# A fourth outer product by seven quarter products: spilled operands, smaller result pieces, half-tile loads

## The chip, the cores and the metric

The kernel runs on one core of one Trainium2 chip. The metric is the device time of one execution in microseconds (us); before the change the median of three runs is 1509.48 us.

## The reference

```python
def reference(x, w):                       # x: 8 x 2048 x 2048 f32, w: 2048 x 2048 f32
    cs = np.cumsum(x, axis=1)
    diff = cs - np.concatenate([zeros((B, 1, D)), cs[:, :-1, :]], axis=1)
    return np.matmul(diff, w).astype(np.float32)
```

The difference of the running sum is x itself, so what has to be computed is x times w: 16384 rows by 2048 times 2048 by 2048.

## The kernel before, in words

The 16384 rows are 128 tiles of 128 rows. The first four tiles are multiplied plainly in bf16 while w is loaded (lines 207 to 389). The other 124 are taken in 31 groups of four: tiles g, g+1, h = g+2 and h+1. A tile of x is loaded by SP (`bring`, line 97), measured by ACT with an absolute sum (`measure`, `weigh`, `weigh_in`), scaled to f16 in place by ACT (`narrow`, line 114), and transposed by a DMA that SP starts (`turn_over`, line 124), whole for even tiles and by two halves for odd ones.

Within a group two levels of Winograd's form of Strassen's scheme are at work.

- The outer level takes the row pair (g, g+1) as the two row halves of a 2 x 2 block product, with K and N halved to 1024. Its seven products are A11 x B11, A12 x B21, S4 x B22, A22 x T4, S1 x T1, S2 x T2 and S3 x T3. S1 to S4 are sums of blocks of x, made by DVE (`total`, line 510) in f16; T1 to T4 are differences of blocks of w, made once. The pair (h, h+1) has the same products. A product of one pair is 16 matmuls of 128x128 by 128x512, so a product for both pairs is 32.
- The inner level takes one outer product for both pairs at once, g and h being its two row halves of 128 rows, and cuts K and N again to 512. It needs seven quarter products of 4 matmuls instead of eight: 28 matmuls in place of 32. Its operands on the side of x are made by DVE each group (`sums_in`); those on the side of w are made once and kept in SBUF (`less_in`, tile `inner`, the lists Q1 to Q4 and t11 to t22).

Before the change three of the seven outer products are made by quarter products in groups 2 to 31: A12 x B21 (`in2`), S4 x B22 (`in3`) and A22 x T4 (`in4`). Four are direct: 4 x 32 + 3 x 28 = 212 matmuls in a group. The first group (`group_plain`) makes all seven directly, 224.

PSUM has eight banks of 128x512. A product is gathered in a bank and then taken out, scaled by its row's factor, into a piece of the result in SBUF: the first one by ACT (`keep`, line 497), the others added by DVE (`add`, line 502). Before, such a piece is 128x1024 f32 and there are four of them (`new_c`); a finished one is stored by SP (`put`, line 507). ABS passes of ACT throw their elementwise output into a free piece (line 105) or a bank (line 553).

The order of each engine's instructions is the order of the program text: `after` (line 134) ties every ACT, DVE and SP instruction behind the last one asked for on the same engine. Matmuls of the groups are asked for without `after`, and stand in the order of the text too. PE writes a bank again only when the instruction that takes it out is done; that wait is a semaphore.

Of the kernel before, what the change touches and what calls it, by code (L numbers as in the profile page):

```python
# [7 lines left out]

# [3 lines left out]
def kernel(  # L34
# [31 lines left out]
    KQ = KO // 4  # L66

    x2 = x.rearrange("b s d -> (b s) d")
    out2 = out.rearrange("b s d -> (b s) d")


# [11 lines left out]
    wmax = const.tile([P, 2 * KO], f32, name="wmax")  # L83
    wred = const.tile([P, 1], f32, name="wred")
# [3 lines left out]
    fin = ctx.enter_context(tc.tile_pool(name="fin", bufs=2))  # L88
    small = ctx.enter_context(tc.tile_pool(name="small", bufs=6))
    xtpool = ctx.enter_context(tc.tile_pool(name="xT", bufs=2))  # L90
# [4 lines left out]


    def bring(t):
        xf = fin.tile([P, K], f32, name="fin")
        return xf, nc.sync.dma_start(xf, x2[ds(t * P, P), :])

    def measure(xf, waste):
        m = small.tile([P, 1], f32, name="m")
        return m, nc.scalar.activation(  # L105
            waste.bitcast(f16), xf, ABS, scale=1.0 / ROW, accum_out=m
        )

    def invert(m):
        s = small.tile([P, 1], f32, name="s")  # L110
        nc.vector.tensor_scalar(m, m, TINY, None, MAX)  # L111
        return s, nc.vector.reciprocal(s, m)  # L112

    def narrow(xf, s):
        xh = xf.bitcast(f16)[:, :K]
        return xh, nc.scalar.activation(xh, xf, COPY, scale=s)  # L116


    def place(t):
        if t % 2 == 0:  # L120
            return [xtpool.tile([P, KO, P], f16, name="xT")]
        return [xtpool.tile([P, KH, P], f16, name=f"xT{h}") for h in range(2)]

    def turn_over(xT, xh):
        n = K // len(xT)
        return [
            nc.sync.dma_start_transpose(a, xh[:, ds(i * n, n)])
            for i, a in enumerate(xT)
        ][-1]

# [12 lines left out]

    with tc.tile_pool(name="ring", bufs=7) as ring, tc.tile_pool(
        name="o", bufs=7
    ) as opool, tc.tile_pool(name="first", bufs=1) as first:
        xP = first.tile([P, PLAIN, KO, P], bf16, name="xP")
        eye = first.tile([P, P], bf16, name="eye")
        zeros = xP[:, 0, :KQ, :].rearrange("p k m -> p (k m)")

# [74 lines left out]

# [19 lines left out]
        def plain_out(h, r):  # L245
            for n in here(h, r):
                if h == 0 or r > 0:
                    c = opool.tile([P, NB], f32, name="o")
                else:
                    c = ring.tile([P, NH], bf16, name="wb").bitcast(f32)  # L250
                after("act", lambda: nc.scalar.copy(c, ps[r][n]))
                done.append((c, ds(r * P, P), ds(h * NH + n * NB, NB)))
# [66 lines left out]
        x4, _ = after("sp", lambda: bring(PLAIN))  # L319
        x6, _ = after("sp", lambda: bring(PLAIN + 2))  # L320
# [23 lines left out]

        waste = first.tile([P, NH], f16, name="waste")
        got = {}
        scales = {}

        def measure_2(t, xf):
            m, m2 = (small.tile([P, n], f32, name=i) for n, i in ((1, "m"), (2, "m2")))  # L350
            for i in range(2):
                at = ds(i * NH, NH)
                after(
                    "act",
                    lambda: nc.scalar.activation(
                        waste, xf[:, at], ABS, scale=1.0 / ROW, accum_out=m2[:, i : i + 1]
                    ),
                )
            after("dve", lambda: nc.vector.tensor_reduce(m, m2, AX.X, ADD))
            scales[t], _ = after("dve", lambda: invert(m))  # L360
            got[t] = m, None

        def narrow_turn(t, xf):
            xh, _ = after("act", lambda: narrow(xf, scales[t]))
            xT = place(t)
            got[t] = got[t][0], xT
            return after("sp", lambda: turn_over(xT, xh))
# [25 lines left out]
        measure_2(PLAIN, x4)  # L393
        for k in range(4, KH):
            block(B11, 0, 0, k, "dve")
        narrow_turn(PLAIN, x4)
# [3 lines left out]
        measure_2(PLAIN + 2, x6)  # L400
        finish_row(1)
        there = xP.rearrange("p r k m -> p (r k m)")
        x5 = there[:, : 2 * K].bitcast(f32)
        after("sp", lambda: nc.sync.dma_start(x5, x2[ds((PLAIN + 1) * P, P), :]))
        narrow_turn(PLAIN + 2, x6)
# [7 lines left out]
        for c, rows, columns in done:  # L413
            after("sp", lambda: put(c, rows, columns, nc.sync))
        m = small.tile([P, 1], f32, name="m")
        after(
            "act",
            lambda: nc.scalar.activation(
                there[:, ds(2 * K, K)].bitcast(f16), x5, ABS, scale=1.0 / ROW, accum_out=m
            ),  # L420
        )
        scales[PLAIN + 1], _ = after("dve", lambda: invert(m))
        got[PLAIN + 1] = m, None
        narrow_turn(PLAIN + 1, x5)
        x7, _ = after("sp", lambda: bring(PLAIN + 3))
# [23 lines left out]

    S1, S2, S4g, S4h, S0 = (Part(B12[j]) for j in range(5))  # L450
    cpool = ctx.enter_context(tc.tile_pool(name="C", bufs=1))
    inpool = ctx.enter_context(tc.tile_pool(name="inner", bufs=1))
    inner = inpool.tile([P, 30, NB], f16, name="inner")
    spare = [inner[:, j, :] for j in range(30)]
    spare += [B12[k][:, n, :] for k in range(5, KH) for n in range(2)]


    def quarters(b):
        return *([spare.pop() for _ in range(4)] for _ in range(3)), *(
            [t[:, n, :] for t in b[4 * a : 4 * a + 4]] for a in range(2) for n in range(2)  # L460
        )

    in2, in3, in4 = quarters(B21), quarters(B22), quarters(T4)

    def product(ps, a, b, first):
        for k in range(KH):
            for n in range(NH // NB):
                nc.tensor.matmul(  # L468
                    ps[n],
                    a[k],  # L470
                    b[k][:, n, :],
                    start=(first and k == 0),
                    stop=(k == KH - 1),
                    skip_group_check=True,
                )

    def product_in(ps, a, b, first):
        for k in range(4):
            nc.tensor.matmul(  # L479
                ps, a[k], b[k], start=(first and k == 0), stop=(k == 3), skip_group_check=True  # L480
            )

    def both(ps):
        return ps.unsqueeze(1).to_broadcast([P, 2, NB])

    def halves(c):
        return c.rearrange("p (n c) -> p n c", c=NB)


    def pieces_of(dst, ps):  # L490
        if isinstance(ps, list):
            return [(dst[:, ds(n * NB, NB)], ps[n]) for n in range(2)]
        return [(dst, ps)]

    def keep(dst, ps, scale):
        for c, p in pieces_of(dst, ps):
            after("act", lambda: nc.scalar.activation(c, p, COPY, scale=scale))  # L497

    def add(dst, ps, scale):
        for c, p in pieces_of(dst, ps):  # L500
            after(
                "dve", lambda: nc.vector.scalar_tensor_tensor(c, p, scale, c, MUL, ADD)  # L502
            )

    def put(c, t, h):
        after(
            "sp", lambda: nc.sync.dma_start(out2[ds(t * P, P), ds(h * NH, NH)], c)
        )

    def total(dst, p, q, op):  # L510
        after("dve", lambda: nc.vector.tensor_tensor(dst.all, p.all, q.all, op))  # L511
# [5 lines left out]

    def less_in(Q1, Q2, Q4, t11, t12, t21, t22):
        less(Q1, t12, t11)
        less(Q2, t22, Q1)  # L520
        less(Q4, t21, Q2)

    def less_in3(Q1, Q2, Q4, t11, t12, t21, t22):
        less(t12, t22, t12)

    def new_c(slot):
        return cpool.tile([P, NH], f32, name=f"c{slot}")

    END = M // P
    came = {PLAIN + 3: x7}  # L530
    units = {}

    def fetch_x(t):
        if t < END:
            came[t], _ = after("sp", lambda: bring(t))

    def weigh(t, slot):
        if t < END:
            xf = came.pop(t)
            m, _ = after("act", lambda: measure(xf, new_c(slot)))  # L540
            got[t] = m, None, xf


    def weigh_in(t, ps):
        if t < END:
            xf = came.pop(t)
            m = small.tile([P, 1], f32, name="m")
            m4 = small.tile([P, 4], f32, name="m4")
            for i in range(4):
                at = ds(i * NB, NB)  # L550
                after(
                    "act",
                    lambda: nc.scalar.activation(  # L553
                        ps[i % 2],
                        xf[:, at],
                        ABS,
                        scale=1.0 / ROW,
                        accum_out=m4[:, i : i + 1],
                    ),
                )  # L560
            after("dve", lambda: nc.vector.tensor_reduce(m, m4, AX.X, ADD))  # L561
            got[t] = m, None, xf

    def scale_of(t):
        if t < END:
            m, _, xf = got[t]
            s, _ = after("dve", lambda: invert(m))
            came[t] = xf, s
# [373 lines left out]
```

## Time and profile before

| | |
|---|---|
| median of 3 runs (lowest, highest) | 1509.48 us (1509.03, 1510.4) |
| span of the profiled execution | 1507.3 us (the profile gives no other time for that execution) |
| matmuls | 6911, PE busy 1490.6 us |
| DVE busy | 1104.4 us in 2053 instructions |
| ACT busy | 864.5 us in 1107 instructions |
| DMA | 351.50 MB, mean 233 GB/s; the hardware queue of SP 81.1% of 16 engines' time |
| HBM read, written | 150.99 MB, 134.22 MB |
| transposes by DMA | 186, started by SP; 5.2 us from start to landing |

A busy time is the union of an engine's instructions; starting a transfer isn't counted as busy on the engine that starts it, but it holds that engine's queue. A group of instructions is written as line, engine, operation, output<-input. In a row of the timeline the first two numbers are the start and the time taken, in us from the span's start.

### The profile page before, as it was taken

What the parts mean: (1) busy time and instruction counts of PE and PEld (TensorE: products, weight loads), DVE (VectorE), ACT (ScalarE), POOL (GpSimd) and SP (SyncE); (2) the same over time, 40 slices, a digit from 0 to 9 for tenths busy, and PEclk for the clock granted to TensorE, in tenths of its full rate; (3) what the DMA queues carried; (4) which work ended last, traced back from release to release, by engine and by line L of the source; (5) the groups of instructions that cost most, each with busy time, mean ns of one, the idle gap of its engine ahead of it and who ended that gap; (6) DMA issues with size and microseconds to landing.
All of it is one profiled execution on the core that took longest, in us unless ns stands there. A gap on an engine that the chain in (4) does not pass through costs nothing.

```text
span 1507.3 us, 19123 instructions
## 1 busy us (share of the span) xinstructions
PE 1490.6 (99%) x6911; PEld 673.8 (45%) x6911; DVE 1104.4 (73%) x2053; ACT 864.5 (57%) x1107; POOL 5.2 (0%) x12
## 2 busy tenths in 40 slices
PE   8999999999999999999999999999999999999998
PEld 3444444444444444444444444444444444444443
DVE  7997777776677676777676776766776767776767
ACT  5875655565655566555656555655555565556551
POOL 0100000000000000000000000000000000000000
PEclk9999999999999999999999999999999999999999
DMA  9988878878978987888789788878788888887772
GB/s 362 351 250 233 236 224 246 234 213 227 235 225 244 224 224 236 215 246 236 210 229 232 230 241 217 235 222 248 216 244 207 236 221 250 232 236 216 223 208 112
DMA packets 322479, 351.50 MB, mean 233 GB/s; under 512 B 266896, under 2 KB 266896, under 8 KB 306512
## 3 DMA queue, kind: packets, MB, share of 16 engines
q1 hardware_dynamic: 321536, 347.92, 81.1%
q0 software_dynamic: 560, 1.84, 0.3%
q8 instruction: 54, 0.88, 0.2%
q10 hardware_dynamic: 288, 0.52, 0.1%
q14 instruction: 41, 0.34, 0.1%
HBM read 150.99 MB, written 134.22 MB: 189 GB/s over the span
## 4 chain that ended last, share of the span: by engine, by line
PE 88%; DVE 1%; DMA 1%; issue 0%; ACT 0%; DVEq 0%; ACTq 0%; SPq 0%
PE b L468 52%; PE b L479 36%; DVE c L502 1%; DMA fin<-in_x_dram 0%; DMA xT<-fin 0%; DVE W L511 0%; ACT b L553 0%; DVE W L515 0%; ACT c L497 0%; DVEq L937 0%; DVE xT L511 0%; DVE s L112 0%; DVE m L111 0%; DVE u L586 0%; DVE m L561 0%
## 5 line engine op out<-in xcount | busy, mean ns | idle before, releaser
L502 DVE SCALAR_TENSOR_TENSOR c<-b,u,c 128x512 f32<-128x512 f32 (+1 forms) x883 | 675.0, 799 | 234.8 <-ACT c L497 112.8
L497 ACT ACTIVATE c<-b,u 128x512 f32<-128x512 f32 x496 | 314.5, 680 | 265.4 <-PE b L468 170.5
L468 PE MATMUL b<-W,xT 128*128 128x512 f16 x2048 | 462.1, 379 | 0.8 <-ACT c L497 0.8
L468 PE MATMUL b<-W,W 128*128 128x512 f16 x1764 | 411.7, 379 | 1.8 <-ACT c L497 1.5
L105 ACT ACTIVATE c<-fin 128x2048 f16<-128x2048 f32 x92 | 175.7, 1910 | 242.4 <-DMA out_dram<-c 220.5
L468 PEld LDWEIGHTS <-xT 128*128 128x128 f16 x2048 | 200.4, 98 | 242.6 <-issue 1.1
L468 PEld LDWEIGHTS <-W 128*128 128x128 f16 x2016 | 197.2, 98 | 240.2 <-issue 2.1
L116 ACT ACTIVATE fin<-fin,s 128x2048 f16<-128x2048 f32 x123 | 246.3, 2002 | 93.8 <-issue 50.8
L479 PEld LDWEIGHTS <-W 128*128 128x128 f16 x1560 | 152.1, 98 | 187.5 <-issue 2.5
L479 PE MATMUL b<-W,W 128*128 128x512 f16 x810 | 220.0, 379 | 1.0 <-DVE c L502 1.0
L479 PE MATMUL b<-W,xT 128*128 128x512 f16 x720 | 180.0, 379 | 0.0
L479 PE MATMUL b<-inner,W 128*128 128x512 f16 x660 | 176.2, 379 | 0.0
L479 PEld LDWEIGHTS <-xT 128*128 128x128 f16 x960 | 93.9, 98 | 113.3
L561 DVE TENSOR_REDUCE m<-m 128x1 f32<-128x4 f32 x29 | 4.6, 157 | 106.7 <-ACT b L553 106.7
L553 ACT ACTIVATE b<-fin 128x512 f32<-128x512 f32 x116 | 67.8, 585 | 14.5 <-DMA fin<-in_x_dram 14.5
L468 PE MATMUL b<-W 128*128 128x512 f16 x252 | 75.0, 379 | 0.0
L511 DVE TENSOR_TENSOR W<-W,xT 128x1024 f16<-128x1024 f16 x122 | 68.2, 559 | 3.2
L511 DVE TENSOR_TENSOR W<-xT,W 128x1024 f16<-128x1024 f16 x122 | 67.5, 553 | 0.0
L479 PE MATMUL b<-inner,xT 128*128 128x512 f16 x240 | 61.6, 379 | 0.0
L233 PE MATMUL b<-wb,xP 128*128 128x512 bf16 x240 | 55.4, 383 | 5.9 <-ACT wb L216 4.8
L511 DVE TENSOR_TENSOR W<-xT,xT 128x1024 f16<-128x1024 f16 (+1 forms) x92 | 54.8, 596 | 0.0
L111 DVE TENSOR_SCALAR m<-m 128x1 f32<-128x1 f32 x124 | 18.5, 149 | 34.6 <-ACT c L105 33.5
(54 smaller groups left out, 457.9 us busy)
## 6 DMA issues: line engine op xcount, KB each, us to landing
out_dram<-c SPq DMA_DIRECT2D x247, 512.0 KB, 3.1
fin<-in_x_dram SPq DMA_DIRECT2D x123, 1024.0 KB, 5.5
W<-in_w_dram SPq DMA_DIRECT2D x32, 512.0 KB, 9.6
W<-in_x_dram SPq DMA_DIRECT2D x16, 256.0 KB, 7.4
xT<-fin SPq DMA_TRANSPOSE x184, 5.2
out_dram<-o POOLq DMA_DIRECT2D x7, 256.0 KB, 3.9
out_dram<-o SPq DMA_DIRECT2D x7, 256.0 KB, 4.1
xP<-in_x_dram SPq DMA_DIRECT2D x1, 1024.0 KB, 5.1
```

Of the source, the lines that this page charges most:

```text
L105: return m, nc.scalar.activation(waste.bitcast(f16), xf, ABS, scale=1.0 / ROW, accum_out=m)
L111: nc.vector.tensor_scalar(m, m, TINY, None, MAX)
L116: return xh, nc.scalar.activation(xh, xf, COPY, scale=s)
L233: lambda: nc.tensor.matmul(ps[r][n], xP[:, r, ko, :], wb[h, ko][:, ds(n * NB, NB)], start=(ko == 0), stop=(ko == KO - 1),),
L468: nc.tensor.matmul(ps[n], a[k], b[k][:, n, :], start=(first and k == 0), stop=(k == KH - 1), skip_group_check=True,)
L479: nc.tensor.matmul(ps, a[k], b[k], start=(first and k == 0), stop=(k == 3), skip_group_check=True)
L497: after("act", lambda: nc.scalar.activation(c, p, COPY, scale=scale))
L502: "dve", lambda: nc.vector.scalar_tensor_tensor(c, p, scale, c, MUL, ADD)
L511: after("dve", lambda: nc.vector.tensor_tensor(dst.all, p.all, q.all, op))
L553: lambda: nc.scalar.activation(ps[i % 2], xf[:, at], ABS, scale=1.0 / ROW, accum_out=m4[:, i : i + 1],),
L561: after("dve", lambda: nc.vector.tensor_reduce(m, m4, AX.X, ADD))
```

## The change

- From group 4 on (28 groups, `five` in the code), S1 x T1 is also made by seven quarter products (`in_5`): 3 x 32 + 4 x 28 = 208 matmuls. Groups 2 and 3 still have three such products, and their quarter products are ordered anew.
- The operands on the side of w no longer fit: four lists of four quarters (Q4 of the products 2, 4 and 5, and t21 of product 3) lie in DRAM (`spill`) and pass through one buffer `flow` (128x2048 f16, 512 KB), brought four times in a group by SP (`bring_flow`). Four inner operands on the side of x pass through `passing`; several others take the place of blocks that are no longer needed.
- The result is held in seven pieces of 128x512 f32 instead of four of 128x1024; each is stored by itself, 16 stores of 256 KB a group instead of 8 of 512 KB.
- x is loaded by halves into a tile `F` of five halves (8 loads of 512 KB a group instead of 4 of 1 MB), measured and scaled by halves, and transposed by halves; the transposes are started by ACT (`turn`) instead of SP.
- Quarter products, steps of two contraction blocks of S2 x T2 and S3 x T3 (`go(P6g)`, `go(P7g)`) and evictions are interleaved in a new order, and matmuls are tied by `after` as well.

The core of the diff, with the new helpers and the new group (X and Y are two banks each, q, e, v and w one each):

```diff
+queue_of_x = [PLAIN, PLAIN + 2, PLAIN + 3]
+for t in range(PLAIN + 4, END, 4):
+    queue_of_x += [t, t + 2, t + 1, t + 3]
+for i, t in enumerate(queue_of_x):
+    where[t] = [F[:, i % 3, :], F[:, 3 + i % 2, :]]
...
+def turn(t, halves=range(2)):
+    if t < END:
+        for i in halves:
+            after(
+                "act",
+                lambda: nc.scalar.dma_start_transpose(
+                    place(t)[i], narrowed(t)[:, ds(i * NH, NH)]
+                ),
+            )
...
-inner = inpool.tile([P, 30, NB], f16, name="inner")
+inner = inpool.tile([P, 24, NB], f16, name="inner")
+flow = inpool.tile([P, 4, NB], f16, name="flow")
+spill = [spills.tile([P, 4, NB], f16, name=f"spill{i}") for i in range(4)]
+free = [cpool.tile([P, NB], f32, name=f"c{i}") for i in range(7)]
...
+def bring_flow(i):
+    after("sp", lambda: nc.sync.dma_start(flow, spill[i]))
...
+def put(c, t, at):
+    after("sp", lambda: nc.sync.dma_start(out2[ds(t * P, P), ds(at * NB, NB)], c))
+    free.append(c)
...
+product(X, A11g, B11, True)            # slots 0 to 3
...
+keeps(C11g, X, ug)
+product(Y, A11h, B11, True)            # 4 to 7
+keeps(C11h, Y, uh)
+weigh(next_g)
+quarter(q, a11, Q.t11, True)           # 8
+add(C11g[0], q, ug)
+quarter(e, s1, Q.Q1, True)             # 9
+add(C11h[1], e, uh)
+quarter(v, a12, Q.t21, True)           # 10
...
+quarter(q, s2, Q.Q2, False)            # 11
+add(C11g[1], q, ug)
+quarter(e, s4, Q.t22, False)           # 12
+add(C11g[1], e, ug)
...
+total(S1h, A21h, A22h, ADD)
+total(S3h, A11h, A21h, SUB)
+scale_of(next_g)
+narrow(next_g)
+total(S2h, S1h, A11h, SUB)
+go(P6g, 2)                             # 13, 14
+quarter(q, s3, Q.Q3, False)            # 15
...
+weigh(next_h)
...
+go(P6g, 2)                             # 16, 17
+keeps(C12g, X, ug)
+turn(next_g, [0])
+quarter(q, a22, Q.Q4, False)           # 18
+add(C11h[0], q, uh)
+put(C11h[0], h, 0)
+bring_flow(3)
...
+scale_of(next_h)
+narrow(next_h)
...
+go(P6h, 4)                             # 19 to 22
+keeps(C12h, Y, uh)
...
+go(P7g)                                # 23
+quarter(v, a12, N.t21, True)           # 24
+keep(C22g[0], v, vg)
+quarter(q, a11, N.t11, True)           # 25
...
+weigh(next_k)
+go(P7g)                                # 26
+quarter(w, b11, R.t11, True)           # 27
+add(C12g[0], w, ug)
+quarter(v, b12, passed, False)         # 28, passed lies in flow
+bring_flow(1)
...                                     # 29 to 43
+quarter(w, r3, R.Q3, False)            # 44
...
+quarter(q, a11, Q.t11, True)           # 45
+keep(C21g[0], q, vg)
+turn(next_h, [1])
+quarter(X[0], a12, Q.t21, False)       # 46
...
+narrow(next_l, [0])
+quarter(e, s1, Q.Q1, True)             # 47
+keep(C21g[1], e, vg)
+keep(C21h[1], e, vh)
+narrow(next_l, [1])
+quarter(X[1], s4, Q.t22, False)        # 48
+turn(next_k, [1])
+turn(next_l, [0])
+quarter(q, s2, Q.Q2, False)            # 49
+add(C21g[1], q, vg)
+add(C21g[1], X[1], vg)
+put(C21g[1], g + 1, 1)
+add(C21h[1], Y[1], vh)
+quarter(Y[0], a22, Q.Q4, False)        # 50
+keep(C21h[0], Y[0], vh)
+quarter(q, s3, Q.Q3, False)            # 51
+add(C21h[1], q, vh)
...
+turn(next_l, [1])
```

The numbers behind the matmul lines are counted here in fours of matmuls from the group's first one.

## The prediction

> **What bounds the kernel now.** I read the engine table first, then the chain, then one steady group by window, its waits, and the queue that starts the transfers.
>
> ```profile
> PE 1490.6 (99%) x6911; PEld 673.8 (45%) x6911; DVE 1104.4 (73%) x2053; ACT 864.5 (57%) x1107; POOL 5.2 (0%) x12
> PEclk9999999999999999999999999999999999999999
> DMA  9988878878978987888789788878788888887772
> ...
> PE 88%; DVE 1%; DMA 1%; issue 0%; ACT 0%; DVEq 0%; ACTq 0%; SPq 0%
> ```
>
> PE fills the span and carries 88% of the chain; its clock is granted in full. So only a matmul removed, or a wait added on PE, can move the time. Windows of one group of four row tiles (columns: busy us and count by engine, clock, DMA share, GB/s):
>
> ```profile
> 726.62:772.42 45.80, 45.80 (x213) 20.69 (x212) 32.95 (x62) 26.24 (x35) 0.00 (x0) 1.00 0.85 227
> 1413.62:1459.42 45.80, 45.80 (x213) 20.76 (x212) 32.95 (x62) 26.23 (x35) 0.00 (x0) 1.00 0.80 239
> ```
>
> Every group takes 45.80 us for 212 matmuls, with no PE idle: 0.216 us a matmul. DVE has 12.9 us to spare, ACT 19.6, DMA 15 to 20%. These are what the change spends. Now SP's queue in that group, which starts the transposes today:
>
> ```profile
> 742.64 3.23 SPq L127 DMA_TRANSPOSE xT<-fin  x1
> ...
> 750.04 4.41 SPq L127 DMA_TRANSPOSE xT<-fin  x1
> ...
> 765.59 2.98 SPq L127 DMA_TRANSPOSE xT<-fin  x2
> ...
> 774.23 1.99 SPq L127 DMA_TRANSPOSE xT<-fin  x1
> ```
>
> Starting a transpose holds the queue for 1.2 to 5.2 us (median 1.95 over the run; 463 us in all, 15 a group). Lastly the end of the last group, where PE does wait:
>
> ```profile
> 1499.28 2.07 DVE L502 SCALAR_TENSOR_TENSOR c<-b,u,c 128x512 f32<-128x512 f32 x3 [0.81 <-PE b L479]
> ...
> 1501.40 0.38 PE L479 MATMUL b<-W,W 128*128 128x512 f16 x1 [0.50 <-DVE c L502]
> ```
>
> The last quarter product adds onto bank q, so it waits until DVE has read q; one other quarter product lies between.
>
> **Part 1, matmuls removed: -24.2 us.** In 28 of the 31 groups S1 x T1 for both row pairs falls from 32 matmuls to 28 (the instruction orders agree: 6911 to 6799). All of them lie on the path: 112 x 0.216 = 24.2. A quarter product (4 matmuls, 0.864 us) is my unit below, "slot"; such a group shrinks from 53 slots to 52, 44.9 us. I count slots from its first matmul.
>
> **Part 2, the one-slot gap on q: +0.14 us a group.** Each group now ends as the old last one did: S2 onto q (slot 49), Y0 (50), S3 onto q (51). From rows: DVE starts 0.42 us after the start of the last matmul before it (743.53 to 743.95), takes 0.75, and PE follows 0.05 after it (1501.35 to 1501.40): 1.22. Undisturbed, PE would start after 5 matmuls, 1.08. So 0.14 a group even with DVE free. In the old tail two queued adds made it 0.5. In the other places I find two slots or more between a read and the next write of a bank.
>
> **Part 3, ACT.** Sixteen evictions a group stay (0.60 us apart, 9.6). ABS by halves: 1.18 each (60.65 to 61.83 in the start), 8 make 9.4; scaling by halves about 1.1 (the 128x1024 ACTIVATE of line 341 is 1.14), 8.8. Together 27.8, against 26.2 now. New are 8 half transposes to start. A half with nothing queued ahead took 1.23 to 1.65; the second of a pair behind two 512 KB stores 3.1 to 4.4. I take 1.4, since ACT's own ring holds nothing but transposes and most of the eight stand 3 us or more apart: 11 us. That is 39 of 44.9. Part of it hides: ACT's queue runs ahead of its arithmetic (the wait for line 116 began at 745.45, the pass before it ran to 747.25), so a transpose can be started while the instruction before it still computes. What is queued behind a transpose is the point, at two places:
>
> - Slots 13 to 28. e's second quarter ends at slot 13 (11.4 us with the 0.42), DVE adds it (12.2), forms two sums (0.61 apart) and the scale: 13.9. ACT scales tile g+4 (to 16.1), measures h+4 (18.4), evicts C12g (19.6; PE wants that bank at slot 23, 19.9), starts a transpose from 18.5 to 19.9, scales h+4 (20.0 to 22.2), evicts C12h (23.5) and v (24.1). PE writes v again at slot 28, 24.2. Margin 0.1; I charge 0.1.
> - Slots 46 to 51. Evict q (39.9 to 40.6), transpose (39.95 to 41.35), half a scaling (42.4), evict e into C21g (43.0). DVE's add of q to the same C21g can begin at 43.35 (slot 50). Margin 0.35, so with 1.4 us the wait stays that of part 2; I charge 0.06 for scatter.
>
> With part 2: 0.30 us a group, 28 x 0.30 = 8.4. Bounds: 0 (if the ends of matmuls are modelled late) and, with a transpose start of 3.2, 0.14 + 1.45 = 1.6 at the second place alone.
>
> A rule here: "DMA: Bandwidth & Descriptors" in the Trainium skill, section "Issuing engines are not separate DMA queues", holds that the time to initiate a DMA "is usually small relative to the DMA itself". By it the moved starts would cost ACT nothing worth counting and the sum would lose the 0.16 us of part 3, 4.5 us in all. The trace disagrees for transposes: median 1.95 us on the queue, 5.1 to landing.
>
> **Part 4, DVE.** 35 adds (0.71 apart by the group's 18.4 us for 26), 8 sums of 1024 (5.5), 16 of 512 (0.40, 6.4), 12 small ones (1.9): 38.6 of 44.9, from 32.95. The closest place is the add of e (C12h0) before slot 47: a run of adds from 28.7 us ends at 40.2, PE wants e at 40.56. Nothing charged; if that cover fails, each 0.1 us is 2.8 us.
>
> **Part 5, transfers.** A group moves 4 x 512 KB more through the flow buffer, 2.1 MB on 10.5. Mean packet times in the trace: 8192 B 430 ns, 4096 B 169, 2048 B 92, transposes' 256 B 25. Today: 512 x 430 + 1024 x 169 + 8192 x 25, over 16 engines, 37 us. After: x by halves 1024 x 169, C 2048 x 92, transposes as now, flow 512 x 169: 10.8 + 11.8 + 12.7 + 5.4 = 40.7, 0.91 of the group. The tightest is the flow before slot 28: its buffer is free at slot 19, issue about 17.4, wanted at 24.2, 6.8 us; loads and stores land in 3.1 to 5.5 today. The seven C pieces are each reused at least 3 us after their store starts. Nothing charged. SP's 28 plain starts take 0.33 each, 9 us; a transpose's wait on ACT no longer blocks them, but loads wait there for transposes to land, about 6.7 us into the next group, before the first store is due (10.4).
>
> A rule that speaks against the change: the same page, "Rules for kernel authors", wants at least 1 MiB per DMA for bandwidth. By it all pieces here are too small and the DMA share would rise past 0.91. The packet rows say the reverse for x: two of 4096 B take 338 ns, one of 8192 B 430.
>
> **Part 6, start and three unconverted groups: +2 us (0 to 6).** Sixteen half transposes move to ACT in the first 130 us (1.24 to 1.4 each, about 20 us), where ACT is busy about 70% of the time (66.4 us of the first 90) and PE already waited 2.3 us for its evictions.
>
> **Sum.** From the profiled span: 1507.3 - 24.2 + 8.4 + 2 = 1493.5. The median of the runs, 1509.48, lies 2.2 us over that span (the execution's own time beside its span is not in the profile); I carry that: 1495.7, say 1496.
>
> **Rivals.**
> - *Everything is hidden* (the waits of parts 2 and 3 vanish into DVE's and ACT's slack): 1509.5 - 24.2 + 0.5, about 1486. For it: all budgets fit. Against: the 1.22 us of part 2 stand in the rows.
> - *ACT's transposes take PE's place as the bound* (slower): if a start on ACT lasts 3.2 us, as many do on SP, the eviction of e at slot 48 is late and PE loses 1.6 us a group against 0.86 gained: 1509.5 + 2 + 28 x 0.74 = 1532. It decides from 0.14 + (t - 1.75) = 0.79, t = 2.4 us. For it: median start 1.95, many at 3 to 4.4 now. Against: those had plain transfers ahead of them on the same queue.
> - *Flow late* (slower): if a 512 KB flow lands in 9.6 us, as W's loads did when DMA was 0.98 busy, PE loses 2.8 us a group: 1509.5 + 2 + 28 x 1.94 = 1566. Against: 0.91, not 0.98, and landings of 3.1 to 5.5 at 0.85.
>
> That the change does not do what it says is excluded by the count of matmuls.
>
> **Chances.** Forecast 0.50 (its own range 1489 to 1505), all hidden 0.20, ACT 0.22 (1507 to 1550), flow 0.08. A measurement here can tell about 0.2%, 3 us, from no change. Faster: 0.48 + 0.20 + 0.02 (a mild ACT case) = 0.70; same: 0.02 + 0.03 + 0.01 = 0.06; the rest, 0.24, slower. Range 1485 to 1526: it leaves out half of the ACT case, most of the flow case and a little below, 0.2 in all.
>
> **What would show it.** Right: groups of 44.9 to 45.5 us, 208 matmuls each; PE idle on the DVE adder just before each group's last quarter; transposes on ACT's queue near 1.4 us; DVE busy near 38.6, DMA near 0.9. Wrong: PE waiting on evictions by ACT, with starts over 2.4 us; PE's first flow quarter waiting for a DMA; or groups over 45.8 us for any reason.

## The result, and the profile after

The changed kernel takes 1808.5 us (median of 4 runs, 1798.89 to 1816.69) against 1509.49 us: a ratio of 1.198, 95% interval 1.1938 to 1.202. Forecast were 1496 us and a range of 1485 to 1526. The profiled execution took 1816.69 us for a span of 1814.9, so 1.8 us lie around the span.

The engine table, clock and DMA slices, two queues and the chain by engine, of the page of the kernel after:

```profile
PE 1559.3 (86%) x6793; PEld 678.8 (37%) x6799; DVE 1228.4 (68%) x2315; ACT 914.3 (50%) x1301; POOL 5.0 (0%) x12
...
PEclk9989898899899899989999989999899998899999
DMA  9977988999999999999999899999999998999994
...
q1 hardware_dynamic: 132624, 345.30, 67.9%
q10 hardware_dynamic: 261888, 65.04, 25.8%
...
DMA 39%; PE 28%; DVE 11%; ACTq 5%; ACT 4%; issue 3%; SPq 0%; DVEq 0%
```

The 112 matmuls are gone, yet PE is busy 69 us longer and now idle for 256 us of the span. DMA carries 39% of the chain, where it had 1%. All transposes sit on a second hardware queue, q10, the ring of ScalarE; everything else that is large stays on SP's ring, q1. One group by window (columns as before), and a short window in it:

```profile
700.00:754.80 54.80, 47.57 (x210) 20.76 (x208) 37.26 (x73) 27.82 (x40) 0.00 (x0) 0.94 0.96 230
734.90:738.00 3.10, 3.10 (x8) 1.16 (x8) 1.74 (x3) 3.07 (x6) 0.00 (x0) 0.50 0.89 309
```

A group takes 54.80 us instead of 45.80 (51 to 65; mean of 28: 55.4), with nearly the matmuls, DVE and ACT that the prediction counted. The second row shows a source of PE's longer busy time: right after a long wait the granted clock is 0.50, and 8 matmuls are begun in 3.10 us. Now the chain of waits of one group, which begins at 713.45:

```profile
712.95 2.60 ACTq L156
715.70 16.00 DMA x<-F
731.73 0.70 DVE inner L502
...
734.89 1.88 PE b L531 x4
736.80 0.76 DVE c L542
738.00 9.27 DMA flow<-spill
747.32 1.04 PE b L531 x4
```

PE is held twice (slots are quarter products of four matmuls, counted from the group's first one, as in the prediction). At slot 18 it waits for DVE's add, which stands behind the sum S1h, and DVE could not form that until a transpose had landed, 16.00 us after its start. At slot 28 it waits for the reload of `flow`, 9.27 us from start to landing. SP's queue in the same group shows how the first makes the second:

```profile
718.18 13.87 SPq L100 DMA_DIRECT2D F<-in_x_dram  x3
732.14 3.06 SPq L553 DMA_DIRECT2D out_dram<-c  x3
735.86 0.34 SPq L100 DMA_DIRECT2D F<-in_x_dram  x1
737.58 0.33 SPq L553 DMA_DIRECT2D out_dram<-c  x1
738.00 0.38 SPq L495 DMA_DIRECT2D flow<-spill  x1
```

Of the three loads in the first row two go out at 718.18 and 719.13; the third waits until the transposes have read `F` and goes out at 731.72. Four stores and a load are queued behind it and go out from 732.14 to 737.58, just ahead of the reload. Finally the transposes by themselves (starting time min/median/max in ns, then landing):

```profile
L156 ACTq DMA_TRANSPOSE x<-F x246: 1246/1344/7067, 66.2 to 1766.4; - x123
...
DMA to landing us min/median/max: 3.0/6.0/22.1
```

and those of the kernel before:

```profile
DMA to landing us min/median/max: 3.2/5.1/8.4
```

It is the last half of a group that is late above all: 6.0 to 19.5 us to landing in the 27 groups that have one, median 16.3 (in e1, below, 5.3 to 8.1, median 6.8).

The distances between starts of matmuls in the trace, less 0.2158 us each, give PE's loss by place, summed over the 28 groups:

| us lost | after | e2 | e1 | e3 | e5 | e6 | e7 | e8 |
|---|---|---|---|---|---|---|---|---|
| before slot 18 | 149.7 | 35.5 | 6.1 | | 1.5 | 1.4 | 2.3 | 2.7 |
| slow matmuls after it | 48.8 | 9.9 | | | | | | |
| before slot 28 | 61.9 | | 8.9 | | 6.1 | 4.7 | 15.4 | 3.9 |
| slow matmuls after it | 20.5 | | | | | | 1.9 | |
| before slot 47 | 1.7 | 1.2 | 13.3 | 8.9 | | | | |
| before slot 50 | | | | | 7.2 | 7.4 | 7.9 | |
| before slot 51 | 6.1 | 5.9 | 6.3 | 6.3 | 20.4 | 20.9 | | |
| all places | 295 | 55 | 35 | 15 | 36 | 35 | 30 | 12 |

(Columns other than after: the experiments below. Empty: under 1 us. The profiled execution of e7 was the slowest of its ten, 1517.83 us for a median of 1511.9, so its column is that of a bad case.) The start and the first three groups lose another 38.6 us against the kernel before: the first group with quarter products of S1 x T1 begins at 257.28 instead of 218.66.

### The profile page after: what moved, and what is told of

It is laid out like the page before. It is cut to its first block, busy times and chain, and to the rows that moved or that the text cites. A ratio compares the mean times of both kernels' runs of the same rounds, so it can differ in the third digit from the quotient of the medians.

```text
span 1814.9 us, 20556 instructions
## 1 busy us (share of the span) xinstructions
PE 1559.3 (86%) x6793; PEld 678.8 (37%) x6799; DVE 1228.4 (68%) x2315; ACT 914.3 (50%) x1301; POOL 5.0 (0%) x12
## 4 chain that ended last, share of the span: by engine, by line
DMA 39%; PE 28%; DVE 11%; ACTq 5%; ACT 4%; issue 3%; SPq 0%; DVEq 0%
DMA x<-F 25%; PE b L531 18%; DMA flow<-spill 13%; PE b L512 10%; DVE c L542 7%; ACTq L156 5%; ACT c L539 2%; DVE x L502 2%; ACT F L143 2%; DVE inner L502 1%; DMA out_dram<-c 1%; SPq L553 0%; DMA F<-in_x_dram 0%; DVE s L131 0%; DVE m L129 0%
## 5 line engine op out<-in xcount | busy, mean ns | idle before, releaser
L542 DVE SCALAR_TENSOR_TENSOR c<-b,u,c 128x512 f32<-128x512 f32 x1048 | 746.6, 746 | 270.7 <-PE b L531 153.1
L512 PE MATMUL b<-W,x 128*128 128x512 f16 x3072 | 759.3, 395 | 5.7 <-ACT c L539 5.2
L539 ACT ACTIVATE c<-b,u 128x512 f32<-128x512 f32 x496 | 316.4, 680 | 507.3 <-PE b L531 317.6
L512 PEld LDWEIGHTS <-x 128*128 128x128 f16 x3072 | 312.6, 102 | 411.1 <-issue 79.6
L143 ACT ACTIVATE F<-F,s 128x1024 f16<-128x1024 f32 x246 | 282.3, 1147 | 277.6 <-DVE s L131 252.4
L531 PE MATMUL b<-W,inner 128*128 128x512 f16 x1392 | 345.3, 385 | 1.9 <-DVE c L542 1.8
L531 PEld LDWEIGHTS <-x 128*128 128x128 f16 x1560 | 153.4, 100 | 428.6 <-issue 170.3
L531 PE MATMUL b<-flow,x 128*128 128x512 f16 x352 | 117.0, 466 | 213.4 <-DVE c L542 155.9
L112 ACT ACTIVATE waste<-F 128x1024 uint8<-128x1024 f32 x246 | 259.4, 1054 | 77.9 <-DMA F<-in_x_dram 73.9
L531 PEld LDWEIGHTS <-inner 128*128 128x128 f16 x1744 | 172.6, 99 | 223.1 <-issue 20.3
L531 PE MATMUL b<-W,x 128*128 128x512 f16 x968 | 234.6, 379 | 3.2 <-DVE c L542 1.7
L502 DVE TENSOR_TENSOR inner<-x,x 128x1024 f16<-128x1024 f16 (+1 forms) x122 | 67.6, 554 | 170.7 <-DMA x<-F 170.7
L502 DVE TENSOR_TENSOR x<-x,x 128x1024 f16<-128x1024 f16 (+1 forms) x214 | 120.4, 574 | 28.7 <-PE b L512 26.1
```

Source lines behind the costliest of these rows:

```text
L112: lambda: nc.scalar.activation(waste, where[t][i], ABS, scale=1.0 / ROW, accum_out=sums_of[t][:, i : i + 1],),
L143: lambda: nc.scalar.activation(narrowed(t)[:, ds(i * NH, NH)], where[t][i], COPY, scale=s),
L512: said = nc.tensor.matmul(to[n], a[k], b[k][:, n, :], start=(first and k == 0), stop=(k == KH - 1), skip_group_check=True,)
L531: said = nc.tensor.matmul(to, a[k], b[k], start=(first and k == 0), stop=(k == 3), skip_group_check=True)
L542: after("dve", lambda: nc.vector.scalar_tensor_tensor(c, p, u, c, MUL, ADD))
```

## Experiments

The main theory is that of the ring: on a ring of their own, a transpose's 256-byte packets take turns with the packets of SP's ring and land late. Its rivals are the traffic of the flow buffer, which the change adds, and ScalarE's order: starts of transposes, and their waits, that hold up the evictions queued behind them.

**e1, e2, e3: the starter, the flow traffic, both.** e1 gives the transposes back to SP:

```diff
-                    "act",
-                    lambda: nc.scalar.dma_start_transpose(
+                    "sp",
+                    lambda: nc.sync.dma_start_transpose(
```

e2 leaves out every reload of `flow` (the quarters read what it last held) and keeps the transposes on ScalarE; e3 does both.

```diff
 def bring_flow(i):
-        after("sp", lambda: nc.sync.dma_start(flow, spill[i]))
+        return
```

> The changed kernel with the half transposes started by SP again, at the same places in the order. Theory A (two rings: a transpose's 256-byte packets on ACT's ring take turns one for one with the 2 to 4 KB packets of SP's ring, so a transpose beside other transfers lands after 10 to 20 us): transposes land in 4 to 8 us, groups of 45 to 47 us, 1490 to 1540 us. Theory B (volume: flow adds 2.1 MB a group and the engines are full whatever the ring): landings stay above 10 us at the group's end, 1760 to 1820 us. Theory C (ACT's queue is held by the starts): also faster, 1490 to 1540, but then the landings need not shorten.

> The changed kernel with the reloads of the flow buffer left out (its quarter products then read whatever lies in it); transposes stay on ACT. Theory A: fewer large packets to take turns with, but loads and stores remain; the last transpose of a group still lands after 9 to 14 us, 1600 to 1740 us. Theory B: the volume is that of before, so 1490 to 1515 us.

> Both edits: transposes started by SP, reloads of the flow buffer left out. Theory A: no more than some 20 us under the run with SP's transposes alone, near 1490 to 1505. Theory B: the same as the run without flow alone, 1490 to 1515. Its distance from the run with SP's transposes alone is the price of the flow traffic once the ring is shared no more.

Measured: e1 1533.8 us, ratio to before 1.0167 (1.0139 to 1.0195); e2 1572.6 us, 1.042 (1.04 to 1.0441); e3 1511.4 us, 1.0014 (1.0003 to 1.0024). The transposes of e1:

```profile
L156 SPq DMA_TRANSPOSE x<-F x246: 1231/1295/4742, 64.6 to 1484.6; - x123
...
DMA to landing us min/median/max: 3.0/3.9/8.1
```

The same instructions, in the same order but for the queue, land in 8.1 us at most, and 275 of the 299 us come back. e2 falls between the two ranges expected: without the flow traffic the slowest landing on ScalarE's ring is still 20.2 us, but PE loses only 35.5 us to it. The two costs are more than their sum: flow is worth 236 us with two rings and 22 us with one. e3 lies 6 us over what the main theory expected, and is no faster than before although it has 112 matmuls fewer and no flow: 15 us stay at slots 47 and 51 and 13.7 us in the start.

**e4: the kernel before, with its transposes started by ScalarE.**

```diff
-            nc.sync.dma_start_transpose(a, xh[:, ds(i * n, n)])
+            nc.scalar.dma_start_transpose(a, xh[:, ds(i * n, n)])
...
-            after("sp", lambda: turn_over(xT, xh))
+            after("act", lambda: turn_over(xT, xh))
```

> The kernel before with its transposes started by ACT, nothing else changed. Theory A: landings rise from 5 us to 8 us or more and the time with them, 1530 to 1700. Theory B: the volume is unchanged, 1508 to 1515. Theory C: ACT's queue is held 15 us a group of its 19.6 us idle, 1510 to 1580 with landings near 5 us.

Measured: 1717.2 us, ratio 1.1379 (1.1356 to 1.1402). The edit alone costs 208 us in a kernel that has neither flow nor smaller pieces, more than any of the three theories expected. But the way is another one. Its transposes:

```profile
L127 ACTq DMA_TRANSPOSE xT<-fin x184: 1247/1624/5907, 65.9 to 1672.8; - x184
...
DMA to landing us min/median/max: 3.2/5.8/8.1
```

And two of ScalarE's waits in the same kernel (us in total, times, longest):

```profile
ACT fin L116 <- issue: 172.1, 30, 7.3
...
ACT c L497 <- issue: 121.9, 25, 6.0
```

The slowest landing is 8.1 us (8.4 on SP). Nor do the starts take longer in all: 14.8 us a group, where they took 15.3 on SP; of a group's six only the second whole tile grew (median 4.56 us against 3.51, up to 5.91). But now they hold ScalarE, which does nothing in the long ones ("issue": nothing else is waited for), and evictions stand behind them. So the same move has two prices: late landings in the changed kernel, starts that hold ScalarE in this one. The waits point to the theory of ScalarE's order here, though its 1510 to 1580 us were too few, and no run takes the 208 us apart. Nor is it tested why two rings leave the landings short here; in the packet records both kinds are under way (over 20 packets of each begun in a us) in 108 of the 1100 us from 300 on, in the changed kernel in 531.

**m1: the two rings by themselves.** A kernel that is no product: two half transposes (2048 packets of 256 bytes) on ScalarE's queue beside six plain transfers on SP's, three rounds of each mix.

```diff
+for i in range(6):
+    nc.sync.dma_start(big[i][:, :cols], x2[ds(i * P, P), ds(0, cols)])
+for d, s in zip(dst, src):
+    nc.scalar.dma_start_transpose(d, s)
```

> Not the product but two half transposes (128x1024 f16) beside plain transfers, in stages with a wait for everything between them; nothing of the reference is computed. Theory A (turns packet by packet between the rings): the pair started by ACT lands in about 3.5 us alone; beside six 512 KB loads on SP's ring in 9 to 14 us, beside six 1 MB loads in 15 to 22, beside six 256 KB loads in 5 to 8, since each 256-byte packet waits for one packet of the other ring; with both on SP's ring and the transposes first, again 3 to 5 us. If the rings shared the engines by bytes or time instead, the pair would land within some 7 us beside loads of any packet size.

Measured, from the start of the pair's first half to the landing of its last: beside six loads of 256 KB (2048-byte packets) 11.4 to 12.4 us; of 1 MB (8192) 18.9 to 19.5; beside six 512 KB stores 16.1 to 17.7. The stage without other transfers and the one with six 512 KB loads (4096) ran into each other, so single halves stand for them: 3.1 us with nothing beside it, 14.2 to 15.4 beside the loads. On SP's own ring behind the loads, a pair's packets take 2.8 to 2.9 us from first to last. All stages together:

```profile
DMA to landing us min/median/max: 3.1/8.7/18.6
```

The delay grows with the size of the other ring's packets, and here with the bytes moved too, so the landings alone do not tell the two apart. The packet records do, for the largest: beside the 1 MB loads 48 to 51 packets of 8192 bytes and 48 to 65 of 256 were begun in each us from 43 to 54, 309 and 18 ns each, close to one for one. Only this mix landed in the range expected; the other loads took longer than the theory of turns expected, and there the large packets were slow as well (4096 bytes: means of 247 to 489 ns in each us from 18 to 25, at best 159).

The changed kernel shows both. In the stretch 728 to 730 us, 99 and 103 packets of 256 bytes and 90 and 89 of 4096 bytes were begun in each us: again close to one for one, 18 and 159 ns each, 392 GB/s in all. But from 716 to 727, the longer part of the 16.00 us above, only 164 GB/s were moved, and a packet of 4096 bytes took 399 ns on average. Turns do not explain that, and no run here shows what does. In the kernel before, on one ring, the transposes run at 1013 packets in the us from 734. The page "DMA: Bandwidth & Descriptors" of the Trainium skill, section "Queues, rings and completion order", says that a DMA engine round-robins between its queue rows at packet granularity, with some 9 to 17 descriptors in a typical packet. The counts agree with turns; whether a packet of the records is a packet or a descriptor of the page, no run here shows. A half transpose has 1024 packets, so at 100 a us it lasts 10 us (an estimate from these counts), where alone it needs little over one. In m1 the slow ring shows in the starts too: beside the 1 MB loads the start of the second half holds ScalarE for 13.1 to 13.3 us, where 1.25 us is the least.

**e5, e6: the order, on SP's ring.** e5 is e1 with a load and the reloads of `flow` put forward, the S2 quarter of A22 x T4 exchanged with that of S4 (so that two slots, not one, lie between DVE's read of bank q and S3's write), and the scale of the last x tile moved behind slot 46. e6 also gives two early outputs a place in `F`, moves the first group's C11h stores forward and measures tile h+5 later.

```diff
-        quarter(X[1], s4, Q.t22, False)
...
         quarter(q, s2, Q.Q2, False)
+        quarter(X[1], s4, Q.t22, False)
...
+        if five:
+            scale_of(next_l)
         narrow(next_l, [0])
```

> Transposes by SP, and in the groups with a fourth inner product five things moved: load(next_l, 0) goes before SP's two transposes, scale_of(next_l) is asked of DVE only at slot 46, the flow reloads 0 and 3 and the last transpose go ahead of stores, and at the group's end S2's quarter comes one slot earlier, so that two slots lie between the writes of q. If the waits left at slots 18, 28, 47 and 51 (0.22, 0.32, 0.47 and 0.22 us a group) come from these orders: groups of 45.0 to 45.5 us and 1508 to 1520 us. If the flow traffic itself is what costs (the engines are 0.95 busy with it): no more than 10 us under the run with SP's transposes alone, 1522 to 1534.

> The kernel before this one, and three edits ahead of the third group: two more pieces of the first four tiles' results go through F instead of the pool of five; C11h is finished earlier in the first group; h+5 is measured earlier. If the 14 us that the start lost against the kernel before are waits for result pieces whose stores have not landed, 6 to 10 us come back: 1498 to 1514 us. If they come from the transfers' volume, nothing comes back.

Measured: e5 1535.2 us, 1.0175 (1.0154 to 1.0195), nothing gained; e6 1524.1 us, 1.01 (1.008 to 1.0119). e5 lies outside both ranges expected. Its slot 47 is free, but slot 51 lost three times as much. Timeline of e6 around slot 51:

```profile
732.19 1.15 ACT L143 ACTIVATE F<-F,s 128x1024 f16<-128x1024 f32 x1 [1.87 <-DVE s L131]
733.25 1.25 ACT L539 ACTIVATE c<-b,u 128x512 f32<-128x512 f32 x2
734.75 1.02 PE L531 MATMUL b<-W,x 128*128 128x512 f16 x4 [0.84 <-DVE c L542]
```

A scaling of ScalarE (L143) waits 1.87 us for its scale, with the two evictions (L539) behind it; DVE's add onto one of those pieces is late, and PE waits for the bank. In e6 the first group takes 49.7 us (e1 58.0, before 50.7), but the second still 54.4 (before 47.2); 7.6 of the start's 14 us come back, as expected if result pieces were waited for (the first group with quarter products of S1 x T1 begins at 225.70, in e5 at 233.28).

**e7, e8: evictions first, then reloads first.** e7 moves both scalings behind the two evictions, and in the first group starts the last tile's transposes ahead of two loads and two stores. e8 moreover issues two of the four reloads of `flow` ahead of a transpose and a load.

```diff
-        narrow(next_l, [0])
         quarter(e, s1, Q.Q1, True)
...
         keep(C21h[1], e, vh)
-        narrow(next_l, [1])
+        narrow(next_l)
```

```diff
-            load(then, 1)
             quarter(q, s3, N.Q3, False)
...
             bring_flow(2)
+            load(then, 1)
```

> The reordered kernel with its transposes on SP and two further edits: in a group's last quarters both narrowings of the last x block stand behind the two evictions of the bank they were queued ahead of, and in the first group the last block's transposes are issued ahead of two loads and two stores. Theory (the 0.75 us a group before slot 51 is ACT's queue held by a narrowing that waits for its scale; the 3.8 us in the second group is the transposes' place on SP): slot 51 falls from 20.9 us over 28 groups to about 6, group 2 from 54.4 to about 49 us, time 1502 to 1509. Rival (the waits are only the visible end of a shortage of DMA time, and move to slots 28 and 50, or to slot 18 through the later transposes of the last block): 1518 to 1526.

> The same with two more edits: two reloads of the flow buffer (those read at slots 28 and 50) are issued ahead of a transpose and a load that stood before them on SP. If the waits at slots 28 and 50 (4.7 and 7.4 us over 28 groups) are the reload's place in the queue, they fall to under 4 us together and the time is 7 to 10 us under that of the run with the evictions first, 1493 to 1501. If they are the share of the transfers' bandwidth, they stay or move, and the two times agree within 4 us.

Measured: e7 1511.9 us (10 runs, 1506.71 to 1517.83), 1.0013 (0.9998 to 1.0028): slot 51 fell to nothing, but slot 28 rose from 4.7 to 15.4 us, as the rival had it in part, and the time lies between the two ranges expected. The second group took 51.9 us, not 49. e8 1497.28 us (1495.44 to 1498.1), 0.9916 (0.99 to 0.9933): the only kernel of the study that beats the one before, by 0.8%, and 14.6 us under e7, where 7 to 10 were expected. PE's waits for the flow buffer in e7 (us in total, times, longest):

```profile
PE b L531 <- DMA flow<-spill: 14.1, 17, 2.3
```

and in e8:

```profile
PE b L531 <- DMA flow<-spill: 2.1, 4, 1.2
```

So the place in the queue, not the bandwidth, made the reloads late. Three lines of the page of e8, then one of its groups by window:

```profile
PE 1472.6 (98%) x6793; PEld 663.0 (44%) x6799; DVE 1227.3 (82%) x2315; ACT 917.8 (61%) x1301; POOL 5.4 (0%) x12
...
PEclk9999999999999999999999999999999999999999
DMA  9999989999999999999999999999999999999994
```

```profile
1400.58:1445.48 44.90, 44.90 (x210) 20.35 (x209) 37.93 (x72) 29.81 (x43) 0.00 (x0) 1.00 1.02 283
```

This group takes 44.90 us at full clock (mean of the 28: 45.3). The records of its packets add up to 1.02 of the DMA engines' time; a sum over 1 means that some overlap.

**e9, e10: one ring or two, in the best order.** e9 is e8 with the transposes started by ScalarE again; e10 is e8 with the transposes on SP and the loads of x started by ScalarE.

```diff
-                lambda: nc.sync.dma_start(
+                lambda: nc.scalar.dma_start(
                     where[t][i], x2[ds(t * P, P), ds(i * NH, NH)]
```

> The fastest kernel so far (transposes on SP, evictions and flow reloads put forward) with the one edit turned back: ScalarE starts the transposes again. If the starter decides alone (ring taking turns with SP's transfers, and ScalarE's own order held by the starts), the most of the 275 us comes back: 1700 to 1800 us, transposes landing in a median of 5 to 6 and a maximum over 15 us. If it was the order of steps, which this kernel has mended, that made the change lose, the time stays under 1540 us.

> The fastest kernel so far, transposes still started by SP, but its loads of x (eight of 512 KB a group) started by ScalarE, so that they have a ring of their own. Theory of the turns by packet: it makes no difference which of the two rings holds the transposes; they meet 4 KB packets of the other ring one for one again, and land in up to 12 to 20 us where the unedited kernel has 3.0, 4.8 and 9.7 us (minimum, median, maximum). Rival (ScalarE's queue is bad for a transpose, not the ring): landings stay at 3 to 10 us. The time says less, since ScalarE then also waits for buffers of x; it rises in either case, by the theory to over 1550 us.

Measured: e9 1757.1 us (six runs, 1729.37 to 1764.63; the profiled one is the fastest), some 1.16 of before; e10 1802.6 us in its one run. Landings of e9, of e10 and of e8, in this order:

```profile
DMA to landing us min/median/max: 3.2/6.7/22.2
```

```profile
DMA to landing us min/median/max: 3.1/6.1/13.5
```

```profile
DMA to landing us min/median/max: 3.0/4.8/9.7
```

e9 settles that order was not what made the change lose: the queue alone costs 232 us (profiled run) to 260 us (median) in the mended kernel. 120.0 of the 213.5 us that PE loses in its 28 groups stand before slot 18 and some 34 in slow matmuls after it; before slot 4, where a bank waits for its eviction by ScalarE, 32.0. e10's slowest landing rises to 13.5 us, in the range expected, and its median by 1.3 us, though SP starts them: 49 of 248 take over 8 us, where 7 do in e8 and 93 in e9. So a second ring is enough to make transposes late, whoever starts them, but here less than in e9. Its time says nothing of the ring: ScalarE's loads wait for transposes to have read `F`, and its evictions behind them (351.2 us in 48 waits).

## Why the prediction was wrong

**The step that failed: part 5, "Nothing charged".** It took landings of 3.1 to 5.5 us and the packet rows from a trace in which all traffic shared one ring, and added packet times as if the ring did not matter. Its 40.7 us were to fill 0.91 of a group of 44.9; the window of 54.80 us has a share of 0.96, so the packets took 52.6 us. That the two shares are close is luck: the same packets took longer, and 230 GB/s were moved, where e8's engines move 283. On one ring the sum was too small as well: 1.02 of 44.90, 45.8 us, in e8. The transposes, moved past SP's queue, were costed as starts on ScalarE and never as transfers. Measured: the last transpose of a group lands 16.3 us after its start (median), which costs 149.7 us before slot 18 and 48.8 us in slow matmuls. That "loads wait there for transposes to land, about 6.7 us into the next group" was seen; in the group shown the last of them waited until 18.3 us into it (731.72 less 713.45).

**Flow before slot 28** was named as the tightest place, 6.8 us from issue to need, and as a rival with 2.8 us a group. Measured: 2.21 us a group, 61.9 in all. The rival's mechanism came about, near its size (the reload shown lands in 9.27 us, 9.6 were supposed); it had a chance of 0.08. It is the smaller part, and in the group shown it follows from the first one (landings of 3.1 to 5.5 us do not hold when two loads and four stores go out in the 6.3 us ahead of it).

**Part 6, start: +2 us (0 to 6)** measured +38.6, and +14.2 in e1, where the ring is not to blame. The small pieces and the late last transposes of the first two groups cost it there, as far as the edits of e6 and e7 show; e8's order brings it to +2.6 (221.22 against 218.66).

**Part 2** was right in kind: PE waits for DVE's add before the last quarter in all 28 groups. 0.22 us a group instead of 0.14, 6.1 us. One exchanged pair of quarters removes it, as e7 and e8 show.

**Part 3** held in its durations: median start 1.344 us against 1.4 taken. Neither of its two places shows among the losses of the kernel after. The rival of ScalarE's starts asked for 2.4 us a start and did not come about here; e4, where some last 5 us, points to it in another kernel.

**Part 4** put DVE at 38.6 us a group; 37.3 in the window. Its closest place, the add before slot 47, did lose 13.3 us once the transposes were back on SP (0.47 a group in e1): DVE stood at a scale whose tile of x had been loaded late, which the budget did not see.

**Part 1** was right: e8's undisturbed groups take 44.90 us, 0.90 less than before, 25 us in 28 groups, for 24.2 forecast. e8 ends 1.3 us from the forecast, but that is another kernel: one queue and the order of a dozen steps stand between them. Of the signs named for a wrong prediction "groups over 45.8 us for any reason" came; the flow quarter that waited for a DMA was not the group's first one (slot 18) but its second (slot 28), and none named a late transpose.

The section of the Trainium skill cited in part 3, "Issuing engines are not separate DMA queues" of "DMA: Bandwidth & Descriptors", speaks of the time to initiate a DMA, and there the trace of after comes nearer to it for halves: a median of 1.344 us against 6.0 to landing. It was read as if the issuing engine made no other difference; e1 shows 275 us of difference, e9 232 to 260.

What stays open: how much of the loss of e9 is ScalarE's held order (the 32 us before slot 4 point to it) and how much comes from landings was not taken apart further; nor why both rings are slow at times, beyond the turns that they take.

## What to carry to other kernels

Before a transfer is moved to another engine's queue, ask what shares the DMA engines with it and in which packet size: here many small packets on a ring of their own got about one turn for each large packet of the other ring, and at times both rings were slower than that. On one ring they are late by what stands ahead of them, which an order of steps can mend. A budget of DMA time that fits says nothing of when a single transfer lands; cost the landing of each transfer that an engine waits for, the last transpose of a stage above all.

## What the runs showed of the hardware

After a wait of several us PE's clock was granted at 0.50 (the window of 3.10 us above): 7 to 14 matmuls start up to 0.43 us apart instead of 0.216. In the kernel after that followed every wait of over 3 us at slots 18 and 28, and none of under 2 us; a mean wait of 5.3 us at slot 18 costs 1.7 us more behind it. Starting a transpose can hold a queue for 5 us and more while nothing else is shown that it waits for (e4: up to 5.9; after: 7.07; m1, behind another half on a slow ring: 13.3). And the packets of 4096 bytes that took 169 ns on average in the kernel before take 235 in the one after and 189 in e8: packet times of one trace are not constants for another.
